# Where the low halves of seven weight tiles are made while the recurrence carries its state

## The chip, the cores and the metric

The kernel runs on one core of a Trainium2 chip. The metric is the time of one execution on the device in microseconds (us). Engines are named as in the profile: PE multiplies matrices (PEld loads its weights beside it), DVE is the vector engine, ACT the scalar engine, POOL is GpSimd, SP issues most DMAs. Each engine takes its instructions in the order in which the program wrote them, and waits at an instruction until its operands are there.

## The reference, cut to what matters

One layer runs on 640 tokens: 512 noisy ones and 128 of a prefix, model width 1024, all in float32.

```python
def _wkv_step(s, inp):
    r, w, k, v, a, b = inp
    sa = jnp.einsum("bhvk,bhk->bhv", s, a)
    s = s * w[:, :, None, :] + sa[..., None] * b[:, :, None, :] + v[..., None] * k[:, :, None, :]
    return s, jnp.einsum("bhvk,bhk->bhv", s, r)

def _trunk_layer(x, cvec, s0, ctx_k, ctx_v, p):
    sh1, sc1, g1, sh2, sc2, g2 = _modulation(cvec, p["w_ada"], p["b_ada"])
    h = _rmsnorm(x, p["norm1_g"]) * (1.0 + sc1) + sh1
    u_rw, u_na, gate_rw, gate_na = jnp.split(h @ p["w_in"], IN_SPLITS, axis=-1)
    o_rw, s_new = _rwkv_branch(u_rw, s0, ...)      # two scans, forward and backward, of _wkv_step
    ...                                            # q, k, v from u_na, o_na = neighbourhood attention
    merged = (jax.nn.sigmoid(gate_rw) * (o_rw @ p["w_o_rwkv"])
              + jax.nn.sigmoid(gate_na) * (o_na @ p["w_o_na"]))
    x = x + g1 * (merged @ p["w_out"])
    h2 = _rmsnorm(x, p["norm2_g"]) * (1.0 + sc2) + sh2
    x = x + g2 * ((jax.nn.silu(h2 @ p["ffn_w1"]) * (h2 @ p["ffn_w3"])) @ p["ffn_w2"])
```

## The kernel before

**Three products for one.** Each float32 operand of a large product is split into a high half (rounded to a type that PE takes at full rate) and the low half that is left. A weight tile of 128x1024 arrives by DMA in `wst`; `wcast` (line 187) makes `whi` by an ACT copy and `wlo` in one of two ways. Way "d": DVE subtracts `whi` from `wst` (line 195). Way "p": ACT writes the negative of `wst`, rounded, into `wlo` (line 190), and a DMA that POOL issues adds `wst` to it (line 191), so that DVE has nothing to do. PE then does high by high, high by low and low by high. A tile of the input projection serves two halves of 320 tokens: 16 products with `whi` and then 8 with `wlo` for each.

**Stages.** Modulation, norm and q, k, v (0 to about 120 us), attention (to about 250), the recurrence (to about 650), the output projection, and the feed-forward net (from about 750). The change lies in the recurrence. It runs over four channel tiles `ct` of 128 channels, each with all its 64-token chunks in both directions:
- `main` builds the triangular systems, `inv` inverts them (DVE's long chain, lines 1286 to 1353);
- `carry` takes the state through eight rounds. A round: PE products L1393, L1405 and L1411; ACT copies their sum to `x` (L1396); PE multiplies by the inverse (L1420); ACT copies the result to `ZV` (L1426); PE products L1433 and L1450; DVE scales to the next `ZV` (L1445), from which the next round starts;
- `out` normalises and gates.

**Work woven in.** PE has room beside all this. A generator `stream` runs the 39 weight tiles of `order` through it (the projections of k, r, v and of the gates, called `k1`, `r1`, `g3` and so on, then the merges `a0` to `b3`): their products are `fl<-h,whi` and `fl<-h,wlo` on line 223. Tables written by hand (`plan`) say how many of these products are put after each step; nothing moves them at run time. The string `wl` has one letter for each tile, "d" or "p". The cast of the next tile is queued (`later`) when an eighth of the present tile's products is written, and the DMA for the tile after that when half is.

During `carry(ct)` another generator, `prep(ct+1)`, is written in between the rounds by `beside`, which takes a queued function first if one is due and charges each against a budget of ACT and DVE time per slot. Its steps are, in this order: a square on ACT (L660), ten small PE products (L664), DVE and POOL for a root (L668, L669), PE products L645 and L647 with an ACT tanh each (L650, L653), transposes (L679) and `kk` on DVE (L682, L684), per direction a scan on DVE (L693, L696) and exponentials on ACT (L702, L707), then the products `NK` and `f` (L721 on ACT, L723, L728, L738, L742 on DVE, L751 on DVE or POOL). What is left of it is written at the last round (`last`, line 1670 on). Then DVE forms `AG` and `R_` for the next channel tile (L1168, L1171), and PE starts the next `main` with L1189, which reads `AG`.

Of the kernel before, what the change touches and what calls it, by code (L numbers as in the profile page):

```python
# [77 lines left out]
    h2=0.91, jobs=((2, 9, 28), (2, 9, 28), (2, 9, 28), (2, 8, 28)),  # L78
    mds=((4, 12), (4, 12), (4, 12), (4, 12)), bud=((1.8, 0.8), (1.3, 1.8)), off=6, tk=2, h3=1,
    h4=1.07, g1=2, km="dddddddd", kb="ddpd", ma="d", yo="pppd", r0="pd", rl=(0, 0, 0), lh=(0, 0, 1, 1),  # L80
    wl="dddddddddppppppppppppppppppppppdddpdddd", nu=9, lg=14, jo=(2, 0, 1), na=(
        "6.0.12.0.1 6.0.12.0.0 6.0.12.0.0 0.0.18.0.2 6.0.12.0.0 6.0.12.0.2 6.0.12.0.0 6.0.12.0.2 6.0.12.0.0 6.0.12.0.2 "
        "6.0.12.1.0 6.1.12.1.2 6.2.12.2.0 6.1.12.0.2 6.2.12.2.0 6.2.12.2.2 6.3.14.2.0 0.0.20.2.2.2 6.2.14.2.0 "
        "0.0.20.0.0 6.5.18.2.0 10.0.10.0.0"))
# [30 lines left out]
def body(ctx: ExitStack, tc: tile.TileContext, xs, xp, cols, consts, w_ada, b_row, w_rw, w_qkv,  # L115
# [26 lines left out]
    def nm(s):  # L142
        cn[0] += 1
        return f"{s}_{cn[0]}"
# [32 lines left out]
    pend, off, hold, gtag = [], [0], [False], ["fl"]  # L177

    def later(fn, cost=(0.5, 0), more=0):
        if off[0]:  # L180
            pend.append([off[0] + more, cost, fn])
        else:
            fn()

    def wcast(w, eng=None):
        st, n, pl, nhl = w
        hi = pl.tile([P, 1024], F32R, tag="whi", bufs=nhl, name=nm("whi"))
        lo = pl.tile([P, 1024], F32R, tag="wlo", bufs=nhl, name=nm("wlo"))
        if eng is pool:
            act.activation(lo[:, :n], st[:, :n], AF.Copy, scale=-1.0)  # L190
            pool.dma_start(lo[:, :n].bitcast(F32), st[:, :n], accum_op=ALU.add)
        act.copy(hi[:, :n], st[:, :n])  # L192
        if eng is not pool:
            def low(a, b):
                dve.tensor_tensor(out=lo[:, a:b], in0=st[:, a:b], in1=hi[:, a:b].bitcast(F32), op=ALU.subtract)  # L195

            if len(gtag) > 1:
                low(0, 512)
                later(lambda: low(512, n), (0, 0), -off[0] + 5)
            else:  # L200
                low(0, n)
        return hi, lo

    def wload(src, eng=None):
        return wcast(wdma(src), eng)
# [22 lines left out]
    def drain(g):  # L228
        for _ in g:
            pass  # L230
# [283 lines left out]
    def tick(n):  # L514
        for p in pend:
            p[0] -= n
        while pend and pend[0][0] <= (-24 if hold[0] else 0):
            pend.pop(0)[2]()
# [261 lines left out]
    def unit(g, e):  # L780

        i, eng = int(g[1:]), eng_of(e)
        if g[0] in "ab":
            return 48 if g[0] == "a" else 36, lambda: merge_load(g[0], i), \
                lambda w: merge_cast(g[0], i, w, eng), lambda w: merge_gen(g[0], i, w)
        if g[0] == "g":
            return 48, lambda: wdma(w_rw[15 + i]), lambda w: wcast(w, eng), \
                lambda w: (gate2_gen if i == PRM["lg"] else gate_gen)(i, w, flps, sb, gtag[-1])
        ci, dst = {"k": (4 + i, kt_), "r": (i, rt_), "v": (8 + i, vp0), "l": (12 + i, lg_)}[g[0]]
        return 48, lambda: wdma(w_rw[ci]), lambda w: wcast(w, eng), \  # L790
            lambda w: proj_gen(ci, dst, flps, sb, "U", len(gtag), w) if g[0] != "l" else lora_gen(i, w)
# [9 lines left out]
    def stream(order):  # L801
        us = [unit(*ge) for ge in zip(order, PRM["wl"])]
        ds, ws = [us[0][1]()], []

        def cast(i):
            if len(ws) == i < len(us):
                ws.append(us[i][2](ds[i]))

        cast(0)
        ds.append(us[1][1]())  # L810
        yield True
        for i, g in enumerate(order):
            while wait.get(g) not in marks:
                yield False
            n, f = us[i][0], us[i][3]
            cast(i)
            it = f(ws[i])
            for j in range(n):
                if j == n // 8:
                    later(lambda i=i: cast(i + 1), (1.05, 0), -off[0])  # L820
                if j == (n // 2 if n == 48 else n // 4) and i + 2 < len(us):
                    ds.append(us[i + 2][1]())
                next(it)
                tick(1)
                if j == n - 1:
                    drain(it)
                    done.add(g)
                    if g == "a0":
                        o_load(4, 6)
                        if "O2" in marks:  # L830
                            o_load(6, 7)
                yield True
# [7 lines left out]
    with s1:  # L840
# [25 lines left out]
        with s1a:  # L866
# [44 lines left out]
            for n in range(12):  # L911
                window(n // 6, n % 6)
            pss = tok_block(pp, (hh, hl), blkch(2), list(range(8)), range(5))
            fill = stream(PRM["order"].split())
            next(fill)
            S = Ct()
# [17 lines left out]
        with ExitStack() as s1b:  # L934
# [128 lines left out]
            with tc.manual_schedule(engines=FIRST):  # L1063
                for k, step in enumerate(PRM["na"].split()):
                    a, p, b, q, n, s_ = (int(x) for x in (step + ".0").split(".")[:6])
# [31 lines left out]
    with ExitStack() as s3:  # L1097
# [403 lines left out]
        def o_load(a, b):  # L1501

            if not o:
                o.extend(Two([]) for _ in range(2))
            for q in sorted(set(range(a, b)) - got):
                got.add(q)
                for i, (t, t_d) in enumerate(zip(o, o_d)):
                    while len(t.ts) <= q // 2:
                        t.ts.append(hp_t("o", i, len(t.ts)))
                    sp.dma_start(t[:, q, :].bitcast(F32), t_d[q])  # L1510
# [498 lines left out]
    with tc.manual_schedule(engines=FIRST):  # L2009
# [5 lines left out]
        for part, fs in enumerate(fts):  # L2015
            old, first, todo = {}, [], [f for f in fs if f >= FA]
# [113 lines left out]
def _build(arrays):  # L2130
    import concourse.bacc as _bacc

    nc = _bacc.Bacc("TRN2", target_bir_lowering=False, num_devices=1)
    args = [nc.dram_tensor(f"in_{n}_dram", v.shape, mybir.dt.from_np(v.dtype), kind="ExternalInput").ap()
            for n, v in arrays.items()]
    args += [nc.dram_tensor(f"out_{i}_dram", s, F32, kind="ExternalOutput").ap()
             for i, s in enumerate(_OUTS)]
    with tile.TileContext(nc, **TCARGS) as tc:
        body(tc, *args)
    return nc  # L2140
# [12 lines left out]
```

## Time and profile before

| | |
|---|---|
| median of 3 runs | 1151.2 us (1149.97 to 1153.36) |
| the profiled execution | 1151.04 us, span 1149.3 us |
| granted TensorE clock | 0.995 of full speed |
| busy share of the span | PE 97%, PEld 86%, DVE 68%, ACT 46%, POOL 17% |
| carry of ct 0, about 298 to 346 us | 48 us: PE busy 46.35, DVE 20.91, ACT 28.45 |
| carry of ct 1, about 394 to 442 us | 48 us: PE busy 46.41, DVE 25.85, ACT 28.53 |
| carry of ct 2, about 492 to 542 us | 50 us: PE busy 48.88, DVE 23.87, ACT 29.21 |
| inv of ct 1, about 346 to 394 us | 48 us: PE busy 47.31, DVE 44.22, ACT 28.25 |

Times in rows of the profile are microseconds from the start of the span, unless marked ns. In a row of the timeline, the two numbers are start and duration, and brackets hold the idle time before it and what ended that. In the chain of work that ended last, each piece is followed by the one that it released. Line numbers are those of the kernel before.

### The profile page before, as it was taken

What the parts mean: (1) busy time and instruction counts of PE and PEld (TensorE: products, weight loads), DVE (VectorE), ACT (ScalarE), POOL (GpSimd) and SP (SyncE); (2) the same over time, 40 slices, a digit from 0 to 9 for tenths busy, and PEclk for the clock granted to TensorE, in tenths of its full rate; (3) what the DMA queues carried; (4) which work ended last, traced back from release to release, by engine and by line L of the source; (5) the groups of instructions that cost most, each with busy time, mean ns of one, the idle gap of its engine ahead of it and who ended that gap; (6) DMA issues with size and microseconds to landing.
All of it is one profiled execution on the core that took longest, in us unless ns stands there. A gap on an engine that the chain in (4) does not pass through costs nothing.

```text
span 1149.3 us, 26860 instructions
## 1 busy us (share of the span) xinstructions
PE 1117.0 (97%) x11160; PEld 990.9 (86%) x11160; DVE 777.8 (68%) x1641; ACT 533.7 (46%) x1052; POOL 195.1 (17%) x262
## 2 busy tenths in 40 slices
PE   6999999999999999999999999999999999999998
PEld 4688878799888888888898788999899989998997
DVE  4565465769558847936787846897478747874775
ACT  4444576665465665456443524654134413441340
POOL 1163244321101212120100421110101010101000
PEclk8999999999999999999999999999999999999999
DMA  9752677654433533343743872222212221232122
GB/s 340 261 113 91 199 277 236 198 153 125 107 75 86 148 85 93 96 119 86 254 122 105 265 213 72 92 93 93 91 56 92 94 90 55 92 97 88 55 91 94
DMA packets 60482, 149.16 MB, mean 130 GB/s; under 512 B 7460, under 2 KB 22436, under 8 KB 60360
## 3 DMA queue, kind: packets, MB, share of 16 engines
q1 hardware_dynamic: 54888, 131.16, 34.7%
q0 software_dynamic: 4032, 14.68, 6.5%
q10 hardware_dynamic: 1440, 1.59, 0.5%
q8 instruction: 88, 1.44, 0.5%
q14 instruction: 34, 0.28, 0.1%
HBM read 118.41 MB, written 14.32 MB: 115 GB/s over the span
## 4 chain that ended last, share of the span: by engine, by line
PE 74%; DVE 10%; issue 8%; ACT 4%; DMA 2%; POOL 1%; SPq 0%; ACTq 0%; DVEq 0%; POOLq 0%
PE acc L311 24%; PE f L1856 21%; PE fl L223 8%; PE mm L223 5%; PE psa L1044 1%; PE lg L959 1%; PE pt L988 1%; DVE RL L1321 1%; DVE pr L1317 1%; PE po L1006 1%; PE w L1420 1%; PE w L1393 1%; DMA o<-o_d 1%; PE w L1433 1%; DMA wlo<-wst 1%
## 5 line engine op out<-in xcount | busy, mean ns | idle before, releaser
L1856 PE MATMUL f<-t,whi 128*128 128x320 f32 x640 | 141.7, 310 | 0.2
L311 PE MATMUL acc<-whi,u 128*128 128x512 f32 (+1 forms) x448 | 136.1, 386 | 0.0
L1856 PE MATMUL f<-b,whi 128*128 128x320 f32 x608 | 135.0, 310 | 0.4 <-DVE b L212 0.4
L223 PE MATMUL fl<-h,whi 128*128 128x320 f32 x672 | 121.4, 321 | 0.0
L1856 PEld LDWEIGHTS f<-t,whi 128*128 128x128 f32 x640 | 106.8, 188 | 0.8 <-issue 0.4
L223 PEld LDWEIGHTS fl<-h,whi 128*128 128x128 f32 x672 | 102.1, 189 | 4.6
L192 ACT CAST whi<-wst 128x1024 fp32r<-128x1024 f32 (+1 forms) x77 | 79.3, 1033 | 52.2 <-PE acc L311 41.5
L1856 PEld LDWEIGHTS f<-b,whi 128*128 128x128 f32 x608 | 101.7, 188 | 1.1 <-issue 0.6
L1856 PE MATMUL f<-t,wlo 128*128 128x320 f32 x320 | 98.9, 309 | 0.0
L311 PEld LDWEIGHTS acc<-whi,u 128*128 128x128 f32 x448 | 83.5, 188 | 16.6
L1856 PE MATMUL f<-b,wlo 128*128 128x320 f32 x304 | 94.1, 309 | 0.0
L1909 ACT CAST whi<-ws 128x1024 fp32r<-128x1024 f32 x40 | 42.0, 1051 | 104.5 <-PE f L1856 45.6
L311 PE MATMUL acc<-wlo,u 128*128 128x512 f32 (+1 forms) x224 | 86.3, 385 | 0.0
L1923 POOL TENSOR_TENSOR ws<-wst 128x512 f32<-128x512 f32 x20 | 29.1, 1454 | 334.7 <-DVE wlo L1912 226.3
L195 DVE TENSOR_TENSOR wlo<-wst,whi 128x1024 fp32r<-128x1024 f32 (+2 forms) x57 | 60.1, 1066 | 30.6 <-ACT whi L192 30.0
L311 PE MATMUL acc<-whi,h 128*128 128x512 f32 x240 | 79.2, 404 | 0.8 <-DVE h L436 0.8
L1724 DVE SCALAR_TENSOR_TENSOR tt<-acc,G 128x512 f32<-128x512 f32 (+1 forms) x51 | 34.7, 680 | 59.0 <-PE acc L311 45.4
L223 PE MATMUL fl<-h,wlo 128*128 128x320 f32 x336 | 63.8, 322 | 0.0
L1909 ACT CAST whi<-wst 128x1024 fp32r<-128x1024 f32 (+1 forms) x48 | 41.3, 869 | 42.3 <-PE acc L311 25.1
L1856 PEld LDWEIGHTS f<-t,wlo 128*128 128x128 f32 x320 | 60.1, 188 | 0.0
L1912 DVE TENSOR_TENSOR wlo<-ws,whi 128x1024 fp32r<-128x1024 f32 x40 | 55.4, 1386 | 5.4 <-ACT whi L1909 5.4
L1445 DVE TENSOR_TENSOR ZV<-w,Dt 64x128 f32<-64x128 f32 x64 | 18.4, 288 | 58.5 <-PE w L1433 57.4
(342 smaller groups left out, 2533.2 us busy)
## 6 DMA issues: line engine op xcount, KB each, us to landing
wst<-in_w_dram SPq DMA_DIRECT2D x66, 512.0 KB
wst<-in_w_rw_dram SPq DMA_DIRECT2D x31, 512.0 KB
wlo<-wst POOLq DMA_DIRECT2D x28, 512.0 KB, 4.7
wa<-in_w_ada_dram SPq DMA_DIRECT2D x24, 512.0 KB
f<-in_w_ada_dram SPq DMA_DIRECT2D x16, 512.0 KB
wst<-in_w_qkv_dram SPq DMA_DIRECT2D x12, 512.0 KB
o<-o_d SPq DMA_DIRECT2D x14, 320.0 KB
x<-in_xs_dram SPq DMA_DIRECT2D x8, 512.0 KB
```

Of the source, the lines that this page charges most:

```text
L192: act.copy(hi[:, :n], st[:, :n])
L195: dve.tensor_tensor(out=lo[:, a:b], in0=st[:, a:b], in1=hi[:, a:b].bitcast(F32), op=ALU.subtract)
L223: pe.matmul(ps[:, :t1 - t0], w[:, a:a + 128], x[:, k0 + kt, t0:t1], start=n == 0, stop=n == 3 * nk - 1)
L311: pe.matmul(pss[i][:, a:b], lhs(x, kt, ts_), w[:, cs_], start=ki == 0 and n == 0, stop=ki == last and n == 2)
L959: pe.matmul(psl[:, hd, o_:o_ + n], qT[ft][rows, qs], x[rows, :], start=True, stop=True)
L988: pe.transpose(pst[:, c * 128:(c + 1) * 128], L[:, c * 128:(c + 1) * 128], ident)
L1445: dve.tensor_tensor(out=V(ZV[own, l + 1, h, :], [[128 * dl, 2], [1, 64]]), in0=V(pn[own, :], [[64, 2], [1, 64]], 64 * g), in1=V(Dt[own, 0, ...
L1724: dve.scalar_tensor_tensor(out=tt, in0=ps[:, a:b], scalar=c, in1=G[:, g, sl], op0=ALU.mult, op1=ALU.mult)
L1856: pe.matmul(ps[:, :H2], w_[:, c_], x_[:, kt, :], start=first and kt + n == 0, stop=last and kt == 3 and n == 2, skip_group_check=more)
L1909: act.copy(r[0][:, :width], src())
L1912: dve.tensor_tensor(out=r[1][:, :width], in0=src(), in1=r[0][:, :width].bitcast(F32), op=ALU.subtract)
L1923: eng_x(PRM["se"][i - 1]).tensor_tensor(out=o_, in0=x, in1=y, op=op)
```

## The change

In the string `wl` seven letters change from "p" to "d": those of `v1`, `g6`, `g7` (cast in the carry of ct 0), `v2`, `g10` (ct 1), `v3` and `g15` (ct 2). For these tiles ACT's negated copy (line 190) and POOL's adding DMA (line 191) are gone. The subtraction on DVE comes in two halves of 512 columns, both queued with `later`: one due 2 products after the cast, one due 4 after it, each charged with 0.7 us of DVE's budget. What has not been taken from the queue when the tile's own products begin is written at that point. Tiles of way "p" elsewhere stay.

```diff
-    wl="dddddddddppppppppppppppppppppppdddpdddd", nu=9, lg=14, jo=(2, 0, 1), na=(
+    wl="dddddddddpppppdddppppddpppppddpdddpdddd", nu=9, lg=14, jo=(2, 0, 1), na=(
...
+    halfs, halving = [], [False]
...
-            if len(gtag) > 1:
+            if halving[0]:
+                todo = [(0, n // 2), (n // 2, n)]
+
+                def piece():
+                    if todo:
+                        low(*todo.pop(0))
+
+                halfs.extend([piece] * 2)
+                for more in (2, 4):
+                    later(piece, (0, 0.7), -off[0] + more)
+            elif len(gtag) > 1:
...
             if len(ws) == i < len(us):
+                halving[0] = len(gtag) == 1 and 0 < i < 31
                 ws.append(us[i][2](ds[i]))
+                halving[0] = False
...
             cast(i)
+            while halfs:
+                halfs.pop()()
             it = f(ws[i])
```

Since casts and pieces are charged against the budget of `beside`, steps of `prep` move too. Three places show how the engines' orders change. Numbers behind names count buffers; the lines of the changed kernel lie 12 (from `proj_gen` on) to 16 (from `stream` on) further down, 2 in `wcast`.

DVE at the end of the carry of ct 0, the last products of `prep` and the start of `AG`, before:

```order
L728 TENSOR_TENSOR NK_4332<-NK_4332,kt__626 128x640
L738 SCALAR_TENSOR_TENSOR f_691_4337<-NK_4332,pre_4065 128x10x64
L742 TENSOR_TENSOR f_691_4337<-NK_4332,pre_4065 128x10x64
L751 TENSOR_TENSOR bv_4329<-bv_4329,NK_4332 128x640
L1168 TENSOR_TENSOR AG<-kk_4002,P_651_4038 64x10x64 x2
L1168 TENSOR_TENSOR AG<-kk_4002,P_672_4180 64x10x64 x2
```

The same place in the changed kernel:

```order
L740 TENSOR_TENSOR NK_4330<-NK_4330,kt__626 128x640
L750 SCALAR_TENSOR_TENSOR f_691_4335<-NK_4330,pre_4065 128x10x64
L754 TENSOR_TENSOR f_691_4335<-NK_4330,pre_4065 128x10x64
L763 TENSOR_TENSOR bv_4327<-bv_4327,NK_4330 128x640
L197 TENSOR_TENSOR wlo_4313<-wst_4167,whi_4312 128x512 x2
L1184 TENSOR_TENSOR AG<-kk_4002,P_651_4038 64x10x64 x2
L1184 TENSOR_TENSOR AG<-kk_4002,P_672_4196 64x10x64 x2
```

The two pieces of `g7` stand between the last product of `prep` and `AG`.

ACT in the last two rounds of the carry of ct 1 (`x_836` and `x_842` are the `x` of the last round but one and of the last; `NK_5803` is the product of the second direction), before:

```order
L747 COPY bv_5769<-NK_5711 128x320 x2
L1396 COPY x_836_5777<-w_5772 128x128
L1426 COPY ZV<-w_5788 64x2x64 x2
L721 ACTIVATE NK_5803<-pre_5580,D 128x320 x2
L1396 COPY x_842_5831<-w_5826 128x128
L545 COPY U_5619<-fl_5744 128x192
```

The same place in the changed kernel:

```order
L1412 COPY x_835_5773<-w_5768 128x128
L1442 COPY ZV<-w_5784 64x2x64 x2
L759 COPY bv_5816<-NK_5744 128x320 x2
L733 ACTIVATE NK_5819<-pre_5580,D 128x320
L1412 COPY x_841_5826<-w_5821 128x128
L733 ACTIVATE NK_5819<-pre_5580,D 128x320
L557 COPY U_5619<-fl_5738 128x192
```

The second half of `NK` for the second direction now stands behind the `x` of the last round.

DVE in the first three rounds of the carry of ct 2 and behind them, before:

```order
L1445 TENSOR_TENSOR ZV<-w_6847,Dt_5372 64x2x64 x4
L668 TENSOR_SCALAR r_944_6981<-w_6975 128x10
L1445 TENSOR_TENSOR ZV<-w_6937,Dt_5372 64x2x64 x2
L1439 TENSOR_TENSOR zf_6833<-w_6937,Dt_5372 128x128
L682 SCALAR_TENSOR_TENSOR kk_7075<-kt__626,C,w_7068 128x512
L684 SCALAR_TENSOR_TENSOR kk_7075<-kt__626,C,w_7069 128x128
L1445 TENSOR_TENSOR ZV<-w_7038,Dt_5372 64x2x64 x2
L693 TENSOR_SCALAR pre_6984<-pre_6984 128x640
```

The same place in the changed kernel:

```order
L1461 TENSOR_TENSOR ZV<-w_6847,Dt_5370 64x2x64 x4
L197 TENSOR_TENSOR wlo_6922<-wst_6818,whi_6921 128x512 x2
L1461 TENSOR_TENSOR ZV<-w_6935,Dt_5370 64x2x64 x2
L1455 TENSOR_TENSOR zf_6833<-w_6935,Dt_5370 128x128
L680 TENSOR_SCALAR r_944_7008<-w_7002 128x10
L1461 TENSOR_TENSOR ZV<-w_7032,Dt_5370 64x2x64 x2
L694 SCALAR_TENSOR_TENSOR kk_7091<-kt__626,C,w_7084 128x512
L696 SCALAR_TENSOR_TENSOR kk_7091<-kt__626,C,w_7085 128x128
L705 TENSOR_SCALAR pre_7011<-pre_7011 128x640
```

Behind the two pieces of `v3`, the root's input and `kk` come one round of `ZV` later; PE's products L664 and L645 to L647, from which they follow, have moved behind L1433, L1450 and six products of line 223 of the second round, and its transposes L679 behind six of the third.

## The prediction

> **What bounds the kernel now.** I read the page first, then the busy time of each engine by windows, PE's waits in the three carries, and last the chain of work and the timeline at the places that the change touches.
>
> ```profile
> PE 1117.0 (97%) x11160; PEld 990.9 (86%) x11160; DVE 777.8 (68%) x1641; ACT 533.7 (46%) x1052; POOL 195.1 (17%) x262
> 298.00:346.00 48.00, 46.35 (x622) 40.61 (x622) 20.91 (x40) 28.45 (x74) 6.12 (x10) 1.00 0.35 89
> 346.00:394.00 48.00, 47.31 (x1016) 44.10 (x1014) 44.22 (x149) 28.25 (x55) 10.50 (x21) 1.00 0.42 108
> ```
>
> The columns of the windows are length, then PE, PEld, DVE, ACT and POOL busy, clock, DMA. PE is nearly full everywhere. In a carry DVE has 27 us of its 48 idle; in the inversion behind it DVE is busy for 44 of 48. DVE's idle time in a carry looks free, and that is what a reader must distrust: it counts where DVE is waited for. What PE waits for in the carries (three answers, carries of ct 0, 1 and 2; total, times, longest):
>
> ```profile
> PE w L1450 <- ACT ZV L1426: 0.7, 1, 0.7
> PE w L1420 <- ACT x L1396: 0.5, 2, 0.3
> PE w L664 <- ACT pre L660: 0.4, 1, 0.4
> ...
> PE w L1420 <- DVE Rt L1364: 0.8, 1, 0.8
> PE w L1420 <- ACT x L1396: 0.4, 1, 0.4
> PE w L664 <- ACT pre L660: 0.2, 1, 0.2
> ...
> PE w L1420 <- ACT x L1396: 0.7, 2, 0.4
> PE w L1433 <- ACT ZV L1426: 0.4, 1, 0.4
> ```
>
> Together 4.1 us, nearly all for ACT: no saving on ACT inside the carries can exceed that. And a PE wait that is avoided counts only if PE does not wait for something else later. So I look at each handover from carry to `main`, where PE's L1189 needs all of `AG`. The end of the carry of ct 0 in the chain that ended last:
>
> ```profile
> 343.43 0.73 DVE bv L751
> 344.17 0.73 DVE AG L1168
> ...
> 347.50 1.44 PE w L1189 x88
> ```
>
> DVE sets this end: its last product `bv` is followed at once by the four parts of `AG`, and `AG` by PE's L1189.
>
> **What the change saves.** Seven ACT copies and seven DMAs go. The DMAs were hidden: PE needs a tile's `wlo` only 16 products into that tile, a tile after its cast, and they land in 4.7 us; the pieces are written before the tile's first product, so no product comes to wait for them, and the staging buffer is free before SP's next load into it, which is written in the middle of the tile. Both I set at nothing. POOL and SP have no other step moved past them. The ACT copies count where they lie ahead of something that PE awaits:
>
> ```profile
> wlo<-wst POOLq DMA_DIRECT2D x28, 512.0 KB, 4.7
> 302.06 1.06 ACT wlo L190
> 304.56 1.28 PE w L664 x10
> 401.20 1.28 PE w L664 x10
> 502.62 1.01 PE w L664 x10
> 421.31 0.45 PE L1420 MATMUL w<-x,Rt 64*64 64x64 f32 x8 [0.44 <-ACT x L1396]
> 522.84 0.45 PE L1420 MATMUL w<-x,Rt 64*64 64x64 f32 x8 [0.31 <-ACT x L1396]
> ```
>
> `v1`: the copy at 302.06 delays L660 and with it PE's L664. Without it the wait of 0.4 goes, and L664, which also stalls for the second half of its operand, takes 1.01 as it does unstalled in the carry of ct 2, not 1.28: 0.4 + 0.27 = 0.7 us. `v2`: 0.2 + 0.27 = 0.5. `g10` and `g15`: 0.44 and 0.31, each as PE waits for an `x` behind the cast. `g6` and `v3`: ACT is waiting there itself, nothing. `g7`: `x` comes 0.3 earlier, but PE then waits as much longer at L1450, since its `ZV` stands behind `NK` on ACT, which waits for DVE: nothing.
>
> **What the change costs.** Fourteen DVE instructions of 512 columns:
>
> ```profile
> L195 DVE TENSOR_TENSOR wlo<-wst,whi 128x1024 fp32r<-128x1024 f32 x37 | 45.0, 1221 | 26.8 <-ACT whi L192 26.3
> L195 DVE TENSOR_TENSOR wlo<-wst,whi 128x512 fp32r<-128x512 f32 x16 | 11.3, 736 | 2.9 <-ACT whi L192 2.9
> 326.56 0.83 ACT L702 ACTIVATE P<-pre 128x320 f32<-128x320 f32 x2
> 323.42 1.49 DVE L696 TENSOR_TENSOR_SCAN pre<-K,pre 128x640 f32<-128x640 f32 x1
> ```
>
> Two pieces cost between one whole tile, 1.22, and twice the row of this size, 1.47; I take 1.35, as pieces back to back overlap a little. For `v1`, `v2`, `v3`, `g10` and `g15` they fall in DVE's waits for the next L1433, and behind them stand L668 or that round's `ZV`, which find DVE free again. For `g6` they push the scan at 323.42 by 1.35, to an end of 326.3, still ahead of 326.56 where ACT takes it up. For `g7` there is no cover: they stand between L751 and `AG`, on the chain shown above. PE's L1189, and DVE's transpose and inversion behind it, come 1.35 later, from which 0.7 was saved before: **ct 0: +0.65.**
>
> The other two handovers lose by the moved steps. End of the carry of ct 1:
>
> ```profile
> 430.82 1.20 ACT L721 ACTIVATE NK<-pre,D 128x320 f32<-128x320 f32 x2
> 432.64 0.83 DVE L728 TENSOR_TENSOR NK<-NK,kt__626 128x640 f32<-128x640 f32 x1
> 433.55 2.08 POOL L751 TENSOR_TENSOR bv<-bv,NK 128x640 f32<-128x640 f32 x1 [12.07 <-DVE NK L728]
> 433.72 0.27 ACT L1396 COPY x<-w 128x128 f32<-128x128 f32 x1 [1.70 <-PE w L1393]
> 434.12 2.20 DVE L742 TENSOR_TENSOR f<-NK,pre 128x640 f32<-128x640 f32 x1
> 438.41 3.37 DVE L1168 TENSOR_TENSOR AG<-kk,P 64x640 f32<-64x640 f32 x4
> ```
>
> Before, both halves of L721 are done at 432.0, when DVE is free for L728. Now the second half stands behind the last round's `x`. That `x` waits for PE; PE is 0.44 early here, so `x` runs at 433.25 to 433.5, the half product (0.6) to 434.1, and L728 starts at 434.12, 1.48 late. Everything behind it on DVE to `AG` follows as before, so `AG` and L1189 come 1.48 later; `g10`'s 0.44 is lost in that wait, `v2`'s 0.5 is kept: **ct 1: +1.0.**
>
> Here a rule bears on the sum. L742 takes 2.20 instead of its median of 0.82 because POOL's L751 runs beside it. The Trainium skill, page "SBUF — State Buffer", section "Who interferes with whom", says that a DVE instruction with two SBUF inputs and a GpSimd one that reads SBUF exclude each other, the second waiting until the first ends. By that rule, the trace agrees, the collision comes again, as both start from L728; were it chance, as rows alone might have it, the tail would lose 1.38 less and the whole sum would be about +0.9.
>
> ```profile
> L742 DVE TENSOR_TENSOR f<-NK,pre x8: 816/822/2196, 234.2 to 535.0; 128x640 f32<-128x640 f32 x8
> ```
>
> End of the carry of ct 2:
>
> ```profile
> 528.53 0.82 ACT L747 COPY bv<-NK 128x320 f32<-128x320 f32 x2
> 532.31 0.55 ACT L1426 COPY ZV<-w 64x128 f32<-64x128 f32 x2 [0.55 <-PE w L1420]
> 533.57 0.83 DVE L728 TENSOR_TENSOR NK<-NK,kt__626 128x640 f32<-128x640 f32 x1 [1.78 <-ACT NK L721]
> 538.69 3.37 DVE L1168 TENSOR_TENSOR AG<-kk,P 64x640 f32<-64x640 f32 x4
> 542.70 1.82 PE L1189 MATMUL w<-AG,f 64*32 64x64 f32 x160
> ```
>
> The transposes L679 come about 1.5 later, so the scan ends 1.0 later, ACT's exponentials and L653 push the next `x`, and PE loses 0.65 in the middle; it gains that back from the waits for `x` (0.31, and 0.4 in the last round). But ACT now does L747 and both halves of the second L721 behind the last `ZV`, which ends as before near 532.8: 532.8 + 0.82 + 1.20 = 534.8, and L728 starts about 1.28 after its 533.57. `AG` ends at 542.06 + 1.28 = 543.34, and PE, which was there at 542.70, waits: **ct 2: +0.65.**
>
> **Sum.** 0.65 + 1.0 + 0.65 = +2.3 us on the profiled 1151.04 (span 1149.3 and 1.74 around it). The profiled execution lies 0.2 under the median of 1151.2; on that the forecast is **1153.5 us**. What follows takes the shift as it is, since PE's L1189 and DVE's inversion (44 of 48 us busy) both start from `AG`.
>
> **Rivals.**
> 1. *Each tail pays whole, nothing is kept (slower).* The mechanism is the DVE and ACT alternation on `NK` at a handover. If the start of the last steps of `prep` is set by `prep`'s own chain and not by PE, then the 0.7 and 0.5 saved on PE are waited away at L1189: 1.47 + 1.48 + 1.28 = +4.2, and +5.6 with one more collision such as that of L742, which costs 1.38. For it: in all three carries the chain runs over DVE or ACT near the end. Against: `prep` itself begins behind L664, which gets earlier. It decides once the tails are over 1.2 us longer than forecast. About 1156.
> 2. *The tails have slack that the chain does not show (not slower).* If PE is kept busy before L1189 and DVE's idle time takes the pieces, what remains is 0.7 + 0.5 + 0.44 + 0.31 = 1.95 saved, 1149.3; if all 4.1 us of waits went, 1147.1. For it: DVE is idle for over half of each carry. Against: PE's wait for `AG` is on the chain at 347.50, and the pieces stand just ahead of it.
>
> **Chances.** Forecast 0.48, with a range of its own from 1152.0 (pieces at 1.22, slack of half a microsecond in two tails) to 1155.3 (pieces at 1.47, both other tails half as long again). Rival 1: 0.37. Rival 2: 0.15. A measurement of this kernel can tell about 0.3%, 3.45 us, from no change: 1147.75 and 1154.65 are the bounds. Rival 1 lies above, and a quarter of the forecast, 0.13: slower 0.50. Of rival 2, 0.06 lies below: faster 0.06. The rest, 0.44, is within. The range that holds 8 in 10 runs from 1150.5, which leaves out most of rival 2, to 1157.0, which holds rival 1 with its collision.
>
> **What would show it.** Right: L664 without a wait in the carries of ct 0 and ct 1 and near 1.0 us long; two pieces of 0.6 to 0.74 ahead of `AG` at the end of the first; a hole on DVE ahead of the second L728 in the other two; waits of PE at L1189 on `AG` of about 1.5, 1.5 and 0.6; again one L742 of over 2 us. Wrong: L1189 no later against the start of its carry than before, or a wait of PE for `wlo`.

## The result, and the profile after

The changed kernel takes 1153.56 us (median of 22 runs, 1150.98 to 1156.75) against 1150.94 us (22 runs) of the kernel before: ratio 1.0022, 95% interval 1.0013 to 1.0031, or +2.5 us (1.5 to 3.6). A second measurement (experiment 10) gave 1.0027 (1.0016 to 1.0039). The change makes the kernel slower by two to three thousandths.

Lines of the changed kernel are 12 higher than before between the split of the weights and the weight stream (L664 is L676, L728 is L740, L742 is L754; L195 is L197), and 16 higher behind it (L1168 is L1184, L1189 is L1205, L1286 is L1302). Engine busy time, the DMA queue that loses seven transfers, and the two windows shown of before:

```profile
PE 1116.3 (97%) x11160; PEld 989.2 (86%) x11160; DVE 787.3 (68%) x1655; ACT 528.2 (46%) x1045; POOL 189.4 (16%) x255
...
q0 software_dynamic: 3024, 11.01, 4.9%
```

```profile
298.00:346.00 48.00, 45.76 (x596) 39.90 (x595) 26.54 (x49) 27.56 (x71) 3.41 (x7) 1.00 0.16 53
346.00:394.00 48.00, 46.13 (x1003) 43.08 (x1004) 43.57 (x149) 26.31 (x52) 9.86 (x20) 1.00 0.43 109
```

DVE has 14 instructions and 9.5 us more, ACT seven instructions and 5.5 us less, queue 0 lost a quarter of its bytes (14.68 MB before). None of these sums is the result, and the windows do not hold quite the same work: the carry of ct 0 begins 1.6 us earlier in this profile, so that more of `AG` falls into its window. PE's waits in the three carries and the start of `main` behind each (windows 298 to 348, 394 to 446 and 492 to 546; total, times, longest):

```profile
PE w L1466 <- ACT ZV L1442: 1.0, 1, 1.0
PE w L1205 <- DVE AG L1184: 1.0, 2, 0.6
...
PE w L1205 <- DVE AG L1184: 1.1, 2, 0.6
PE w L1436 <- DVE Rt L1380: 0.8, 1, 0.8
...
PE w L1436 <- ACT x L1412: 0.8, 1, 0.8
PE w L1205 <- DVE AG L1184: 0.5, 1, 0.5
```

The waits at L676 for ACT are gone, and behind each carry PE now waits for DVE's `AG`, where the kernel before has no such wait in the same windows. The end of the carry of ct 0 on DVE, with the two pieces ahead of `AG`:

```profile
341.09 0.82 DVE L763 TENSOR_TENSOR bv<-bv,NK 128x640 f32<-128x640 f32 x1
341.82 1.28 DVE L197 TENSOR_TENSOR wlo<-wst,whi 128x512 fp32r<-128x512 f32 x2
343.02 3.36 DVE L1184 TENSOR_TENSOR AG<-kk,P 64x640 f32<-64x640 f32 x4
```

The ends of the other two carries (the timeline of the changed kernel): DVE, two ACT rows ahead of it in each, and PE's L1205 in ct 2:

```profile
432.25 0.27 ACT L1412 COPY x<-w 128x128 f32<-128x128 f32 x1 [1.39 <-PE w L1409]
432.41 0.66 ACT L733 ACTIVATE NK<-pre,D 128x320 f32<-128x320 f32 x1
433.10 0.82 DVE L740 TENSOR_TENSOR NK<-NK,kt__626 128x640 f32<-128x640 f32 x1 [1.10 <-ACT NK L733]
...
434.57 2.17 DVE L754 TENSOR_TENSOR f<-NK,pre 128x640 f32<-128x640 f32 x1
...
532.84 0.82 ACT L759 COPY bv<-NK 128x320 f32<-128x320 f32 x2
533.70 1.20 ACT L733 ACTIVATE NK<-pre,D 128x320 f32<-128x320 f32 x2
...
534.93 0.82 DVE L740 TENSOR_TENSOR NK<-NK,kt__626 128x640 f32<-128x640 f32 x1 [0.41 <-ACT NK L733]
...
543.48 1.77 PE L1205 MATMUL w<-AG,f 64*32 64x64 f32 x154 [0.51 <-DVE AG L1184]
```

In ct 1 the second half of `NK` now stands behind the last `x`, and DVE has the forecast hole of 1.10 in front of L740; L754 is long again, 2.17. In ct 2 the hole says nothing: it is 0.41, and before it was 1.78. There the sign is ACT, which does L759 and both halves of the second L733 behind the last `ZV`, to 534.90, and L740 follows.

Absolute times shift from run to run, so I compare a stretch: from a carry's first L1433 on PE to the transpose L1286 on DVE that opens the next inversion. For ct 1 the kernel before has these two rows:

```profile
398.74 0.69 PE L1433 MATMUL w<-ZV,TG 128*64 128x64 f32 x16
...
446.20 1.25 DVE L1286 STREAM_TRANSPOSE RL<-Nt 128x1024 f32<-128x1024 f32 x1 [2.83 <-ACT Nt L1194]
```

and the changed kernel these:

```profile
398.44 0.69 PE L1449 MATMUL w<-ZV,TG 128*64 128x64 f32 x16
...
446.62 1.25 DVE L1302 STREAM_TRANSPOSE RL<-Nt 128x1024 f32<-128x1024 f32 x1 [2.83 <-ACT Nt L1210]
```

47.46 and 48.18: +0.72. The table has all stretches, read from the same two rows in each profile, their sum against the kernel before, and the timed difference with its interval (the ratio on 1151 us). The numbers are those of the experiments; kernel 2 is the kernel of experiment 2, and so on.

| kernel | ct 0 | ct 1 | ct 2 | sum, against before | timed, against before |
|---|---|---|---|---|---|
| before | 48.80 | 47.46 | 51.39 | | |
| changed | 49.32 | 48.18 | 51.96 | +1.81 | +2.5 (1.5 to 3.6) |
| 1 pieces uncharged | 49.52 | 46.29 | 50.84 | -1.00 | +0.6 (-0.7 to 1.7) |
| 2 and g7 behind `AG` | 48.34 | 46.30 | 50.83 | -2.18 | -2.6 (-4.1 to -1.0) |
| 3 changed, g7 three times | 52.80 | 48.18 | 51.97 | +5.30 | +6.7 (5.2 to 8.1) |
| 4 changed, covered ones twice | 49.71 | 48.41 | 51.97 | +2.44 | +4.1 (2.6 to 5.8) |
| 5 uncharged, ACT copy kept | 50.00 | 47.45 | 51.40 | +1.20 | +2.5 (1.2 to 3.9) |
| 6 moved steps alone | 48.61 | 49.33 | 52.53 | +2.82 | +4.8 (3.2 to 6.4) |
| 7 before, `bv` on DVE | 48.78 | 47.07 | 51.41 | -0.39 | +0.8 (-0.5 to 2.0) |
| 8 as 2, `bv` on DVE | 48.32 | 45.92 | 50.84 | -2.57 | -1.4 (-2.6 to 0.0) |
| 9 before again | 48.81 | 47.44 | 51.38 | -0.02 | +0.3 (-1.0 to 1.8) |
| 10 changed again | 49.32 | 48.18 | 51.95 | +1.80 | +3.1 (1.8 to 4.5) |
| 11 kernel 2 again | 48.32 | 46.31 | 50.82 | -2.20 | -0.9 (-2.3 to 0.6) |

These three stretches of one program repeat to 0.02 us from one profile to the next (9, 10 and 11), which the times do not by far. Other stretches need not: from the transpose of ct 0 to the first L1433 of ct 1 the two profiles of the kernel before have 46.94 and 47.69.

### The profile page after: what moved, and what is told of

The parts are those of the page before. It is cut to its first block, busy times and chain, and to the rows that moved or that the text cites. A ratio compares the mean times of both kernels' runs of the same rounds, so it can differ in the third digit from the quotient of the medians.

```text
span 1151.0 us, 26846 instructions
## 1 busy us (share of the span) xinstructions
PE 1116.3 (97%) x11160; PEld 989.2 (86%) x11160; DVE 787.3 (68%) x1655; ACT 528.2 (46%) x1045; POOL 189.4 (16%) x255
## 3 DMA queue, kind: packets, MB, share of 16 engines
q10 hardware_dynamic: 1440, 1.59, 0.5%
## 4 chain that ended last, share of the span: by engine, by line
PE 75%; DVE 11%; issue 8%; ACT 3%; DMA 2%; POOL 1%; SPq 0%; DVEq 0%; ACTq 0%; POOLq 0%
PE acc L323 24%; PE f L1872 23%; PE fl L235 8%; PE mm L235 5%; PE psa L1060 1%; PE lg L975 1%; PE pt L1004 1%; DVE RL L1337 1%; DVE pr L1333 1%; PE po L1022 1%; DVE AG L1184 1%; DVE Rt L1369 1%; PE w L1449 1%; PE w L1436 1%; PE w L1409 1%
## 5 line engine op out<-in xcount | busy, mean ns | idle before, releaser
L197 DVE TENSOR_TENSOR wlo<-wst,whi 128x1024 fp32r<-128x1024 f32 (+2 forms) x71 | 69.4, 992 | 33.7 <-ACT whi L194 32.9
L1872 PEld LDWEIGHTS f<-b,wlo 128*128 128x128 f32 x304 | 57.1, 188 | 0.1
```

The costliest lines, as they stand in the source:

```text
L1872: pe.matmul(ps[:, :H2], w_[:, c_], x_[:, kt, :], start=first and kt + n == 0, stop=last and kt == 3 and n == 2, skip_group_check=more)
```

## The experiments

### 1. Order restored: pieces that cost the queue nothing

```diff
-                    later(piece, (0, 0.7), -off[0] + more)
+                    later(piece, (0, 0), -off[0] + more)
```

> Edit: the pieces cost the order of the carry's side work 0 in place of 0.7, so no other step is moved; the pieces stay where they are. Theory (the tails of the carries of ct 1 and ct 2 lose by the moved steps, ct 0 by the two pieces of g7): ct 0 +0.65, ct 1 -0.94 (0.5 of v2 and 0.44 of g10 kept), ct 2 -0.31 (g15): -0.6 us against the kernel before, 2.9 under the changed one; the second NK product of the carries of ct 1 and ct 2 is back at its old distance from AG. Rival (the pieces themselves, wherever they stand, push DVE and with it the three handovers): no change against the changed kernel, about +2.5 us against the one before.

Measured: 1151.34 against 1151.10, ratio 1.0005 (0.9994 to 1.0015). That excludes +2.5, the rival; the stretches give +0.72, -1.17 and -0.55, where the theory had +0.65, -0.94 and -0.31. In ct 1 the second half of `NK` no longer stands behind the last `x`, and L740 follows DVE's `ZV` without a hole:

```profile
430.94 0.61 DVE L1461 TENSOR_TENSOR ZV<-w,Dt 64x128 f32<-64x128 f32 x2 [1.89 <-PE w L1449]
431.58 0.83 DVE L740 TENSOR_TENSOR NK<-NK,kt__626 128x640 f32<-128x640 f32 x1
...
433.06 2.19 DVE L754 TENSOR_TENSOR f<-NK,pre 128x640 f32<-128x640 f32 x1
```

The pieces stand in the same places on DVE in both programs. So the loss of ct 1 and ct 2 comes from the order, and of PE's waits for `AG` only that of ct 0 is left, 1.0.

### 2 and 11. g7's two pieces behind `AG`

```diff
                             akr(S2, d)
+                        while halfs:
+                            halfs.pop()()
```

with the pieces uncharged, and those of `g7` not queued.

> Edit: as the one with uncharged pieces, and the two pieces of g7 are written behind the four parts of AG instead of ahead of them. Theory (what g7 costs is only that AG comes 1.35 later): ct 0 -0.7 where the uncharged one has +0.65, and so -1.95 us against the kernel before. Rival (DVE's 1.35 us only move: the copies and transposes that DVE does behind AG come later by as much, and the inversion with them): -0.6 us, as the uncharged one.

> Edit: none; the kernel with uncharged pieces and g7's pieces behind AG once more, beside the kernel before and the changed one on one chip. By the sum -1.95 us against the kernel before, by the three stretches of its profile -2.2, and so 4 to 4.3 under the changed kernel. Rival (its first result was scatter): 0 against the kernel before.

Measured: 1148.24 (ratio 0.9977, 0.9964 to 0.9991) and again 1149.95 (0.9992, 0.9980 to 1.0005). The first lies below the kernel before and narrowly excludes the rival's -0.6; the second excludes neither that nor no change. That this version beats the kernel before is likely (its stretches are 2.2 shorter both times), not settled by the times. Beside the changed kernel on the same chip (experiment 10: 1154.39) the second is 4.4 us lower, where 4 to 4.3 was forecast. The trace shows why: DVE does the pieces in the time in which it waits for ACT's `Nt` anyway.

```profile
342.01 3.38 DVE L1184 TENSOR_TENSOR AG<-kk,P 64x640 f32<-64x640 f32 x4
345.42 1.29 DVE L197 TENSOR_TENSOR wlo<-wst,whi 128x512 fp32r<-128x512 f32 x2
346.63 1.56 DVE L1187 TENSOR_TENSOR R__2901<-rt__625,P 128x640 f32<-128x640 f32 x2
349.73 1.25 DVE L1302 STREAM_TRANSPOSE RL<-Nt 128x1024 f32<-128x1024 f32 x1 [1.55 <-ACT Nt L1210]
```

The wait before the transpose is 1.55 here; in the changed kernel it is 2.75. PE has no wait for `AG` behind any of the three carries. The stretch of ct 0 is 1.18 shorter than in experiment 1.

### 3. g7's pieces three times

```diff
+                again[0] = 3 if i == 16 else 1
...
-                        low(*todo.pop(0))
+                        ab = todo.pop(0)
+                        for _ in range(n):
+                            low(*ab)
```

with `n` a default of `piece`, bound to `again[0]`.

> Edit: the changed kernel with each of g7's two pieces written three times (the same result, four instructions more, just ahead of AG in the carry of ct 0). Theory (these pieces have no cover): four times 0.60 to 0.68, +2.4 to +2.7 us on the changed kernel, +4.9 to +5.3 against the one before, and AG of ct 0 as much later against the carry's start. Rival (slack behind them: PE is busy, or DVE catches up in the inversion): below +0.5 on the changed kernel, about +3 against the one before.

Measured: 1158.42, ratio 1.0058 (1.0045 to 1.0070): 4.1 us over the changed kernel by the two ratios, with some 1.8 of uncertainty; the rival is excluded. The stretch of ct 0 is 3.48 longer, more than the forecast 2.4 to 2.7.

```profile
343.09 4.19 DVE L197 TENSOR_TENSOR wlo<-wst,whi 128x512 fp32r<-128x512 f32 x6
347.20 3.37 DVE L1187 TENSOR_TENSOR AG<-kk,P 64x640 f32<-64x640 f32 x4
...
355.48 1.25 DVE L1305 STREAM_TRANSPOSE RL<-Nt 128x1024 f32<-128x1024 f32 x1 [3.32 <-ACT Nt L1213]
```

(Lines are 3 higher again.) PE's waits in that carry, their longest group:

```profile
PE w L1208 <- DVE AG L1187: 3.4, 4, 1.8
```

Of the 3.48, 2.91 is the four added pieces, 0.73 each, more than the 0.60 to 0.68 taken. The other 0.57 lies between `AG` and the transpose, 8.28 against 7.71 in the changed kernel. The windows there (length, then PE, PEld, DVE, ACT and POOL busy, clock, DMA) show what else differs:

```profile
346.00:348.00 2.00, 0.23 (x2) 0.00 (x0) 1.97 (x3) 0.97 (x2) 1.32 (x3) 1.00 0.37 107
...
350.00:352.00 2.00, 1.57 (x103) 1.38 (x104) 1.97 (x3) 0.00 (x0) 0.00 (x0) 0.50 0.91 248
...
354.00:356.00 2.00, 2.00 (x18) 1.67 (x14) 0.53 (x1) 1.44 (x3) 0.00 (x0) 0.50 0.24 92
```

While PE waits for `AG` it is busy for 0.23 of 2 us, and behind that the granted clock is 0.50 up to the transpose at 355.48. That is the likely cause of the 0.57, though no run separates it. The mean clock of all six executions is 0.993 or 0.994, against 0.994 to 1.000, 0.998 on average, of the kernel before beside them; so a part of the time that this kernel loses is a lower clock.

### 4. The covered pieces twice

```diff
+                again[0] = 2 if i in (14, 21, 22, 28, 29) else 1
```

with the loop over `n` of experiment 3.

> Edit: the changed kernel with the two pieces of v1, v2, g10, v3 and g15 written twice each (the same result, ten instructions more, some 6.5 us of DVE's time, in the places where DVE waits for the next round). Theory (they lie in DVE's waits): 0 on the changed kernel, at most 0.5, about +2.5 us against the one before. Rival (each tail pays whole: DVE's work is never made up in a carry): +6.5 on the changed kernel, +9 against the one before.

Measured: 1155.33, ratio 1.0036 (1.0023 to 1.0050), 1.6 over the changed kernel with an uncertainty of 1.8. The rival's +6.5 is excluded. The stretches grew by 0.39, 0.23 and 0.01 for ten pieces: the cover is nearly whole. The 0.39 has its row in PE's waits of the carry of ct 0, a wait that is new:

```profile
PE w L1412 <- DVE r L682: 0.3, 1, 0.3
```

A small DVE step between the two pairs of `v1` came late. Single pieces leave it alone.

### 5. The ACT copies kept

```diff
+        if halving[0] and eng is not pool:
+            act.activation(lo[:, :n], st[:, :n], AF.Copy, scale=-1.0)
         act.copy(hi[:, :n], st[:, :n])
```

on top of experiment 1: the old negated copy is written, no DMA adds to it, and the pieces overwrite it.

> Edit: the kernel with uncharged pieces, with the old copy on ACT kept for the seven tiles (its result is overwritten by the pieces; no DMA adds to it). Theory (ACT's copies stood ahead of work that PE awaits): the savings of ct 0 0.7, ct 1 0.5 and 0.44, ct 2 0.31 are gone, 1.95 us over the uncharged kernel, whose own median came 0.24 over the kernel before: about +2.2 us; PE's waits ahead of the projections of pre in the carries of ct 0 and ct 1 are back. Rival (the copies were covered, and the uncharged kernel is better than the changed one by its order alone): as the uncharged kernel, +0.2 to +0.6 us.

Measured: 1152.97, ratio 1.0022 (1.0010 to 1.0034), +2.5 where +2.2 was expected; the rival's +0.2 to +0.6 lies outside the interval. The stretches lose what experiment 1 had kept: 0.48, 1.16 and 0.56, together 2.20 against the 1.95 of the sum. This experiment and the kernel before differ only in the pieces and the adding DMAs: of its +1.20, all but 0.02 is the price of `g7`'s pieces from experiments 1 and 2, so that the other pieces and the DMAs together cost nothing that can be seen. The waits are back where they were (carries of ct 0 and ct 1):

```profile
PE w L678 <- ACT pre L674: 0.4, 1, 0.4
...
PE w L678 <- ACT pre L674: 0.2, 1, 0.2
```

### 6. The moved steps alone

```diff
                 ws.append(us[i][2](ds[i]))
+                if i in (14, 15, 16, 21, 22, 28, 29) and len(gtag) == 1:
+                    for more in (2, 4):
+                        later(lambda: None, (0, 0.7), -off[0] + more)
```

in the kernel before.

> Edit: the kernel before, with two empty entries of the pieces' cost queued for each of the seven tiles: the steps stand where the changed kernel has them, with the old ACT copies and adding DMAs and without pieces. Theory (the moved steps cost the tails of ct 1 and ct 2, and nothing of ct 0): in ct 1 the second NK product waits for the last x, now also 0.44 later: +1.9; in ct 2 0.65 + 0.31: +1.0; together +2.9 us against the kernel before, with AG later by as much against the carry's start. Rival (the moved steps lie in slack; the change's loss is its pieces): 0.

Measured: 1155.90, ratio 1.0042 (1.0028 to 1.0056), +4.8 with a lower end of 3.2: slower than the theory's +2.9, and far from the rival's 0. The stretches give -0.19, +1.87 and +1.14, together +2.82, where 0, 1.9 and 1.0 was expected. DVE at the end of the carry of ct 1, without a single added DVE instruction:

```profile
433.63 0.83 DVE L728 TENSOR_TENSOR NK<-NK,kt__626 128x640 f32<-128x640 f32 x1 [1.10 <-ACT NK L721]
...
435.11 2.17 DVE L742 TENSOR_TENSOR f<-NK,pre 128x640 f32<-128x640 f32 x1
...
439.38 3.37 DVE L1171 TENSOR_TENSOR AG<-kk,P 64x640 f32<-64x640 f32 x4
```

The hole of 1.10 is the changed kernel's, to the hundredth. PE's waits for `AG` are 1.1 behind ct 1 and 0.5 behind ct 2, as in the changed kernel, and there is none behind ct 0.

### 7 and 8. POOL's `bv` moved to DVE

```diff
-    ... kb="ddpd", ...
+    ... kb="dddd", ...
```

in the kernel before (7) and in kernel 2 (8).

> Edit: the kernel before, with the sum bv of the recurrence's preparation for ct 2 on DVE instead of POOL, nothing else. Theory (at the end of the carry of ct 1 the product f takes 2.20 in place of 0.82 because POOL's bv runs beside it): f is back at 0.82, bv adds 0.73 behind it, AG comes 0.65 earlier: -0.65 us against the kernel before. Rival (the long f is set by something else, as the wait for NK or the other readers): f stays near 2.2 and DVE has bv on top: +0.7 us.

> Edit: the kernel with uncharged pieces and g7's two pieces behind AG, and the sum bv of ct 2's preparation on DVE instead of POOL. Theory: both gains add, as they lie in different carries: -2.9 us (what the kernel with g7's pieces behind AG measured against the kernel before) and -0.65: -3.5 us. Rival (PE is the bound by then, and AG of ct 1 is not the last thing that it waits for): -2.9 us.

The mechanism is as the theory has it: without POOL's L751 beside it L742 takes 0.82, in the programs with L751 on POOL it took 2.17 to 2.20 at this place. In experiment 7:

```profile
433.71 0.82 DVE L742 TENSOR_TENSOR f<-NK,pre 128x640 f32<-128x640 f32 x1
434.44 0.82 DVE L751 TENSOR_TENSOR bv<-bv,NK 128x640 f32<-128x640 f32 x1
...
437.36 3.37 DVE L1168 TENSOR_TENSOR AG<-kk,P 64x640 f32<-64x640 f32 x4
```

The gain is smaller than expected: `AG` comes 0.64 earlier, but from `AG` to the transpose it now takes 8.04 instead of 7.79, so 0.39 is left. In the time nothing is to be seen: 1151.61 (ratio 1.0007, 0.9996 to 1.0017), whose lower end, -0.5, just excludes the forecast -0.65; and 1149.38 for kernel 8 (0.9988, 0.9977 to 1.0000), not told apart from kernel 2. The forecast -3.5 and the rival's -2.9 both lie outside its interval, -2.6 to 0.0; its stretches are 0.39 shorter than those of kernel 2. A gain of 0.4 us lies below what these runs resolve, and whether it is lost behind the transpose stays open.

### 9 and 10. The two kernels once more

No edit.

> Edit: none; the kernel before, once more under another name, to see how far the times of one and the same program lie apart. In the profiles so far the stretch from a carry's first product to the transposes behind it repeats to 0.2 us, and yet most experiments came 1.2 us slower than these stretches say. If that is only scatter (short drops of the granted clock), this comes at 0 +/- 1.5 us against the kernel before. If a kernel that is run as the experiment is slower for some other reason, it comes at +1.2.

> Edit: none; the changed kernel once more, on the same chip as the other two. By the sum of the prediction +2.3 us against the kernel before; by the three stretches in its one profile +1.8. Rival (a part of the first result was that chip's): 0 to +1.

Kernel 9 came at 1150.88 against 1151.05 (ratio 1.0003, 0.9991 to 1.0016, or -1.0 to 1.8 us): nearer to no offset for a kernel that is run as the experiment, but the +1.2 of the other case is not excluded. Kernel 10 came at 1154.39 (1.0027, 1.0016 to 1.0039), so the first result repeats, and the rival's 0 to +1 is excluded.

## Why the prediction was right

The forecast of 1153.5 against 1153.56 is nearer than its terms deserve. Its +2.3 is the sum of three parts whose mechanisms the experiments bear out, but each part came out a little lower than forecast, and the stretches give +1.81; the rest of the measured time lies where the forecast had nothing. That the totals agree to a tenth is luck. Experiments 1, 2 and 6 size the parts. "Copies gone" is kernel 2 against before, "g7's pieces" kernel 1 against kernel 2, "moved steps" kernel 6 against before; the forecast terms are in brackets.

| part | ct 0 | ct 1 | ct 2 | sum |
|---|---|---|---|---|
| copies gone | -0.46 (-0.7) | -1.16 (-0.94) | -0.56 (-0.31) | -2.18 (-1.95) |
| g7's pieces | +1.18 (+1.35) | -0.01 (0) | +0.01 (0) | +1.18 (+1.35) |
| moved steps | -0.19 (0) | +1.87 (+1.92) | +1.14 (+0.96) | +2.82 (+2.88) |
| together | +0.53 (+0.65) | +0.70 (+1.0) | +0.59 (+0.65) | +1.82 (+2.3) |
| changed kernel | +0.52 | +0.72 | +0.57 | +1.81 |

The first two rows add up to kernel 1 by their making; that kernel 1 and the moved steps together give the changed kernel's own stretches, within 0.02 us in each carry, is the test, and nothing of size is missing inside the carries.

- **The copies.** The mechanism was right: experiment 5, which puts the copies alone back, loses 2.20. The split was not. In ct 0 the wait of 0.4 went, but L676 did not fall to 1.01; ACT has done both halves at 302.43, and the ten products still take 1.28:

```profile
301.42 1.01 ACT L672 ACTIVATE pre<-kt__626,C 128x320 f32<-128x320 f32 x2
302.50 1.28 PE L676 MATMUL w<-K,pre 128*128 128x2 f32 x10
```

  The 0.27 of that step was therefore a misreading, not a stall for ACT's second half: the 1.01 came from the chain, where a piece begins at the end of the one before it; in the timeline the same ten products of ct 2 take 1.17. In ct 1 the size came out for `v2` all the same: the time from the carry's first L1433 to the L1393 ahead of `g10`'s wait is 20.56 in experiment 1 against 21.07, 0.51 less. To the L1420 behind that wait it is 1.11 less, so `g10` gave 0.60 for 0.44. `v2`, `g10` and `g15` together gave more than forecast, 1.72 against 1.25; why `g10` and `g15` gave more is open. And of the 4.1 us of waits called nearly all for ACT, 0.8 is for DVE's `Rt`.
- **g7's pieces.** No cover, as forecast: two pieces, 1.28 long together, push `AG` and the stretch by 1.18 (experiment 2), a little under the 1.35 taken; four more cost 2.91 ahead of `AG` (experiment 3).
- **The other pieces and the DMAs.** Set at nothing, and rightly: together 0.02 (experiment 5). Doubled pieces cost 0.6 us for ten (experiment 4), and no wait for `wlo` appears.
- **The moved steps.** The largest loss, and the best forecast: 1.87 for 1.92 and 1.14 for 0.96 (experiment 6). The hole ahead of L740 is there in ct 1. In ct 2, where a hole had been there before, the path is right instead: against the carry's first L1433 `AG` comes 1.21 later (1.28 was forecast, though the forecast's own figures give 1.25) and PE's L1205, but for its first six products, 0.62 (0.65). The 0.19 that the moved steps gain in ct 0 was not forecast, and its cause is open.
- **The long L742.** It came again, 2.17. Experiments 7 and 8 show that POOL's L751 makes it: with that on DVE the length is gone. The Trainium skill, page "SBUF — State Buffer", section "Who interferes with whom", says that a DVE instruction with two SBUF inputs contends with a GpSimd one that reads SBUF, and the two experiments agree with it.
- **PE's waits at L1189.** Forecast 1.5, 1.5 and 0.6; shown are 1.0, 1.1 and 0.5, where the kernel before has none. They come and go with the parts: experiment 1 keeps that of ct 0 alone, experiment 6 those of ct 1 and ct 2 alone, kernel 2 none. The path is thereby shown; the first two were forecast 0.5 and 0.4 too long. A wait is not the price: in ct 0 `AG` comes 0.52 later and PE, without the copies, 0.46 earlier, and PE waits for both. The price had to be read as a stretch.
- **The rivals.** That each tail pays whole (+4.2 or more) falls: with the moved steps alone ct 1 loses 1.87, in the changed kernel 0.72, so what the copies save is kept behind a late `AG` too (experiment 6). That the tails have slack falls as well (experiments 3 and 6).

What stays open is the rest between the stretches and the times: +1.8 against +2.5 and +3.1, and 1 to 2 us in the same direction in experiments 1, 3 to 8 and 11; only the first run of kernel 2 lies the other way. Kernel 9 has 0.3, with an interval that does not settle a microsecond. The rest lies outside the three stretches; one candidate is in the last section.

## What to carry to other kernels

Count what an edit does to the order that a queue with costs writes out, not only the instructions that it adds: here charging hidden instructions 0.7 each moved other steps behind the last rounds and cost 2.8 us, more than all fourteen new instructions. On an engine with half its time idle, an instruction costs its whole length where it is put ahead of the step that the next stage waits for, and nothing just behind it, where the engine waits anyway. To size effects of half a microsecond, compare stretches between two fixed instructions in two profiles; those of the carries repeated to 0.02 us where medians of a dozen runs left 1.2. Take a second profile of the same program first to see that the stretch repeats, and look that no drop of the clock falls into it, as one did in experiment 3.

## What the runs showed of the hardware that was not expected

The granted clock drops for short stretches whose place changes from run to run. In experiment 1, the windows behind the last carry (length, then PE, PEld, DVE, ACT and POOL busy, clock, DMA):

```profile
556.00:558.00 2.00, 0.68 (x3) 0.30 (x2) 0.98 (x1) 0.99 (x2) 0.00 (x0) 1.00 1.02 401
558.00:560.00 2.00, 1.47 (x6) 1.25 (x7) 1.23 (x6) 0.00 (x0) 0.00 (x0) 0.81 1.03 405
560.00:562.00 2.00, 2.00 (x9) 1.56 (x8) 0.71 (x2) 0.00 (x0) 0.00 (x0) 0.50 1.05 394
562.00:564.00 2.00, 2.00 (x76) 1.53 (x76) 1.64 (x7) 1.19 (x2) 0.00 (x0) 0.84 1.05 403
```

The clock falls to 0.50 and the loss is 2 x (0.19 + 0.50 + 0.16) = 1.7 us. It comes behind waits of PE for a DMA:

```profile
557.40 0.56 PE L235 MATMUL fl<-o,whi 128*128 128x320 f32 x2 [1.27 <-DMA o<-o_d]
...
558.94 0.41 PE L235 MATMUL fl<-o,whi 128*128 128x320 f32 x1 [0.37 <-DMA o<-o_d]
```

The Trainium skill, page "TensorE: Matmul & The Clock Gate", section "What's actually happening", describes half rate after an idle window of about 3.4 us that runs freely; an estimate from that, half of 3.4, is the 1.7 measured. In this trace PE was busy for 2.15 of the 4.0 us before the deepest drop, so if such a window is the cause here, it was not wholly idle.

A drop behind the waits for `o` stands in five of the thirteen profiles (kernels 1, 3, 4, 7 and 10), all with a longest wait of 1.1 to 1.7. The other eight have 0.3 to 1.0 there, but for kernel 8, which waited 1.54 without a drop. Kernel 6 has its drop earlier, at 548 to 554, behind a wait of 1.59 for ACT, and both profiles of the kernel before have one at 294 to 300, ahead of the first carry's stretch. In experiment 3 a drop that loses 3.4 us follows the waits for `AG`. So these drops come behind idle time of PE, but not every long wait is followed by one, and whether the changed kernels have them more often, and lose the open microsecond by it, thirteen profiles do not settle.
